# A two-layer hybrid block: how the RWKV-7 triangles of the second layer are inverted

## The chip, the cores and the metric

The kernel runs on one core of a Trainium2 chip. The metric is the time of one execution on the device, in microseconds (us), as the median of several runs.

## What is computed

The program is a backbone block of two layers on 256 context tokens and 256 latent tokens of width 1024. Each layer projects its normed input into three parallel mixers (mLSTM, RG-LRU, RWKV-7), gates and sums their outputs, and ends in a SwiGLU network. The part that matters here is the RWKV-7 scan, run over 16 heads of width 64 and in both directions:

```python
def step(s, x_t):
    r_t, w_t, k_t, v_t, kap_t, kapa_t = x_t
    s_kap = jnp.einsum('bhvk,bhk->bhv', s, kap_t)
    s = s * w_t[:, :, None, :] - s_kap[..., None] * kapa_t[:, :, None, :] + v_t[..., None] * k_t[:, :, None, :]
    return s, jnp.einsum('bhvk,bhk->bhv', s, r_t)
```

The latent scan starts from the final state of the context scan. Layer 1 returns both streams; of layer 2 only the latent stream is wanted, so its context half has no outputs.

## The kernel before

**Chunks and units.** The scan is cut into chunks of 32 tokens. Within a chunk the update is a triangular system: a strictly triangular 32x32 matrix per head, direction and chunk has to be inverted, and then a chunk is a few small matmuls. A *unit* u is four heads on one half of the tokens (even u: context, odd u: latent), in both directions, with eight chunks each, so each layer has eight units. Unit 2q+1 starts from the state that unit 2q leaves.

**The steps of a unit.** `rw_load` fetches its projected rows from DRAM. `rw_prep` builds decays and scaled keys, mostly on VectorE (L747 to L760). `chunks` (inside `rw_prep`) multiplies them on TensorE and masks the products into the tile `Am` on VectorE (L782): the triangles. It waits for the end of chain u-2, since `Am` has two buffers. Four or eight DMAs then write the triangles to a scratch in DRAM, `sc1` (L790, L793). `rw_tok` transposes keys and values. A *solve* inverts the triangles and brings the inverses back into `Am`. `rw_chain` then goes through the eight chunks, one after the other, each with a copy `xs` (L1102) near its start; its first instructions wait for the solve. `rw_tail` norms a unit's outputs and writes them.

**Two solves.** `rw_solve32` (layer 1) reads 64 triangles of 32x32, one on each of 64 partitions, and eliminates on GpSimd: for each of 30 columns one multiply (L1031) and one subtract (L1033). One DMA stores the inverse, four bring it into `Am` (L1043). `rw_solve16` (layer 2) reads only the two 16x16 diagonal blocks of each triangle, on 128 partitions, and eliminates 14 columns (L974, L976). A copy transposes one block (L980), two DMAs store, four load the transposed block `PT` (L989) and eight load the blocks into `Am` (L992). Then TensorE makes the missing off-diagonal block: 64 small matmuls of `PT` with `Am`, which the trace counts as 128 (L999), a masked copy `Z` on ScalarE (L1002), 64 matmuls of `Z` with `Am`, again counted as 128 (L1007), and four copies on ScalarE into `Am` (L1012).

**What sets the order.** `weave` (L296 on) is a planner that runs while the program is built. Tasks are generators that yield costs, waits and conditions; the planner keeps a clock of its own and writes out the order of every engine's instructions, SP's DMA queue and GpSimd's among them. The last task of the list is `products`: the large projections for the other mixers (tile `mm`, L260). It fills TensorE wherever no other task is ready, and goes first where fewer than `COLS[l]` matmul columns (3000 in layer 1, 2400 in layer 2) were issued in the last 3413 ns of the planner's clock. Preparations stand ahead of chains, chains ahead of fills. Each engine then runs in exactly that order; an instruction whose data is late holds everything behind it on its engine. In layer 2 about half of the fill products have 256 columns in place of 512.

**The switch.** `BLOCKED[l]` (L38) picks the solve in three places: the stores of the triangles (L788 and L791), the task that is spawned (L794) and the shape of the scratch (L831).

Of the kernel before, what the change touches and what calls it, by code (L numbers as in the profile page):

```python
# [34 lines left out]
COLS = [3000, 2400]  # L35
GDP = 1
ORD = [0, 0]
BLOCKED = [0, 1]  # L38
SL = 1000
SW = 230  # L40
PW = 1700
# [172 lines left out]
class KB:  # L214
# [446 lines left out]
    def rw_prep(self, l, u, ctx_out):  # L661
# [103 lines left out]
        def chunks(bks, sc1):  # L765
# [20 lines left out]
            for j in range(2):  # L786
                for x in range(2):
                    for k in range(2 if BLOCKED[l] else 0):  # L788
                        b = 64 * x + 32 - 32 * j + 16 * k
                        nc.sync.dma_start(out=sc1[k, x, j].rearrange("q s t -> s q t"), in_=Am[b:b + 16, j, :, :, 16 * k:16 * k + 16].rearrange("p d c t -> p (d c) t"))  # L790
                    if not BLOCKED[l]:  # L791
                        b = 64 * x + 32 - 32 * j
                        nc.sync.dma_start(out=sc1[x, j].rearrange("q s t -> s q t"), in_=Am[b:b + 32, j, :, :, 0:32].rearrange("p d c t -> p (d c) t"))  # L793
            yield ("spawn", (self.rw_solve32, self.rw_solve16)[BLOCKED[l]](l, u, Am, sc1))  # L794
            yield ("spawn", self.rw_tok(l, u, ctx_out, bks, bp, v, dict(kr=kr, Am=Am, PL=PL)))
# [34 lines left out]
        self.locks.discard("sm")  # L830
        sc1 = self.dr.tile([2, 2, 2, 16, 16, 16] if BLOCKED[l] else [2, 2, 16, 32, 32], F32, name="sc1")  # L831
        bks = [None, None]
# [1095 lines left out]
```

## Time and profile before

| | us |
|---|---|
| median of 3 runs | 2859.28 (2857.77 to 2861.8) |
| the profiled execution | 2865.19 |
| its span in the trace | 2863.5 |
| TensorE busy | 2669.4 (93%) |
| VectorE busy | 1733.0 (61%) |
| ScalarE busy | 1280.4 (45%) |
| GpSimd busy | 604.4 (21%) |

The span is the time from the first to the last instruction of the program in the trace. PE is TensorE, DVE VectorE, ACT ScalarE, POOL GpSimd, SP the engine whose queue issues most DMAs. A busy TensorE is not TensorE at its peak, since matmuls are pipelined and the time of one is counted from its start to its modelled end. PEclk is the granted share of TensorE's full clock of 2.4 GHz; it has two levels, 1.00 and 0.50, and a stretch shows their mean.

### The profile page before, as it was taken

Reading aid. Unit: us, or ns where it says so; the run is one execution under the profiler, and the core shown is the slowest. Engines: PE = TensorE matmul, PEld = TensorE weight load, DVE = VectorE, ACT = ScalarE, POOL = GpSimd, SP = SyncE. Lnnn points to the kernel's source line nnn. Section 1 sums busy time; section 2 is a strip of 40 time slices with the busy share of each in tenths; the row PEclk is TensorE's granted clock in tenths of the full one; section 3 lists DMA queues with packets and bytes.
Section 4 is the critical chain, followed back from the end, with each engine's and each line's share of the span. In section 5 each row is a group of like instructions: output and inputs, shape, how many; then the busy total and the mean of one; then the engine's idle time right before and its main releaser. Section 6 shows DMA issues by size and latency. Waiting matters only on the chain.

```text
span 2863.5 us, 75206 instructions
## 1 busy us (share of the span) xinstructions
PE 2669.4 (93%) x31560; PEld 2056.4 (72%) x31560; DVE 1733.0 (61%) x3762; ACT 1280.4 (45%) x2536; POOL 604.4 (21%) x983
## 2 busy tenths in 40 slices
PE   6998999999988999999999999999989998889998
PEld 4876677666644676777777877777767675589898
DVE  4677777785678524553333366656566567767564
ACT  4544444443377422342222254444444337755553
POOL 1056666565022000020000010222322201100000
PEclk9999999999999999999999999998999998999999
DMA  6543343434452557755554345433334345377564
GB/s 218 181 131 112 113 114 117 112 105 115 155 159 91 191 162 227 229 187 155 169 166 143 120 135 162 140 96 97 100 106 109 88 152 162 98 219 234 148 183 141
DMA packets 253716, 418.18 MB, mean 146 GB/s; under 512 B 95904, under 2 KB 145824, under 8 KB 253376
## 3 DMA queue, kind: packets, MB, share of 16 engines
q1 hardware_dynamic: 231344, 336.75, 38.7%
q10 hardware_dynamic: 22032, 76.61, 9.4%
q8 instruction: 248, 4.06, 0.6%
q14 instruction: 92, 0.75, 0.1%
HBM read 347.18 MB, written 65.04 MB: 144 GB/s over the span
## 4 chain that ended last, share of the span: by engine, by line
PE 70%; DVE 11%; DMA 7%; issue 5%; ACT 4%; POOL 3%; SPq 1%; ACTq 0%; POOLq 0%; DVEq 0%
PE mm L425 23%; PE mm L260 20%; PE mm L1591 8%; PE sm L260 6%; DMA wraw<-in_wA_dram 3%; PE sm L1429 2%; PE u L260 2%; PE sc L260 2%; PE xy L260 2%; PE xy L1248 2%; DVE wlo L473 1%; DMA yraw<-ysc 1%; PE sm L1525 1%; PE u L1550 1%; PE u L441 1%
## 5 line engine op out<-in xcount | busy, mean ns | idle before, releaser
L260 PE MATMUL mm<-hl,whi 128*128 128x512 f32 (+1 forms) x1184 | 456.4, 385 | 10.9 <-DVE stage L549 9.1
L260 PE MATMUL mm<-hh,whi 128*128 128x512 f32 (+1 forms) x1184 | 458.7, 387 | 0.0
L260 PE MATMUL mm<-hh,wlo 128*128 128x512 f32 (+1 forms) x1184 | 457.6, 386 | 0.3 <-issue 0.3
L383 DVE TENSOR_TENSOR wlo<-wraw,whi 128x512 fp32r<-128x512 f32 (+1 forms) x310 | 214.2, 694 | 287.0 <-ACT whi L382 283.9
L425 PE MATMUL mm<-hl,whi 128*128 128x512 f32 (+1 forms) x1056 | 368.6, 349 | 9.1 <-ACT whi L382 7.1
L425 PE MATMUL mm<-hh,wlo 128*128 128x512 f32 (+1 forms) x1056 | 362.0, 344 | 11.4 <-DVE wlo L383 11.3
L425 PE MATMUL mm<-hh,whi 128*128 128x512 f32 (+1 forms) x1056 | 360.7, 342 | 0.0
L382 ACT CAST whi<-wraw 128x512 fp32r<-128x512 f32 (+1 forms) x310 | 188.4, 614 | 346.0 <-PE mm L425 236.4
L473 DVE TENSOR_TENSOR wlo<-wraw,whi 128x512 fp32r<-128x512 f32 x296 | 225.8, 764 | 82.6 <-ACT whi L470 79.5
L260 PEld LDWEIGHTS mm<-hl,whi 128*128 128x128 f32 x1184 | 227.9, 192 | 60.2 <-issue 7.8
L260 PEld LDWEIGHTS mm<-hh,wlo 128*128 128x128 f32 x1184 | 227.9, 192 | 45.0 <-issue 3.1
L260 PEld LDWEIGHTS mm<-hh,whi 128*128 128x128 f32 x1184 | 227.9, 193 | 43.7 <-issue 1.0
L382 ACT CAST whi<-wx 128x512 fp32r<-128x512 f32 x212 | 128.8, 609 | 266.1 <-PE mm L425 164.7
L470 ACT CAST whi<-wraw 128x512 fp32r<-128x512 f32 x296 | 182.1, 617 | 139.4 <-PE mm L260 98.2
L425 PEld LDWEIGHTS mm<-hl,whi 128*128 128x128 f32 x1056 | 202.0, 191 | 58.5 <-ACT whi L382 25.5
L383 DVE TENSOR_TENSOR wlo<-wx,whi 128x512 fp32r<-128x512 f32 x212 | 144.6, 683 | 148.8 <-ACT whi L382 146.9
L425 PEld LDWEIGHTS mm<-hh,wlo 128*128 128x128 f32 x1056 | 201.8, 191 | 45.7 <-DVE wlo L383 13.7
L1277 POOL TENSOR_TENSOR nsq<-nsq,stage 128x256 f32<-128x256 f32 (+1 forms) x28 | 25.9, 926 | 954.1 <-ACT stage L1275 698.2
L425 PEld LDWEIGHTS mm<-hh,whi 128*128 128x128 f32 x1056 | 202.1, 191 | 22.9 <-issue 2.9
L1591 PE MATMUL mm<-ylo,whi 128*128 128x256 f32 (+1 forms) x544 | 183.7, 338 | 4.0 <-DVE ylo L383 3.8
L1591 PE MATMUL mm<-yhi,wlo 128*128 128x256 f32 (+1 forms) x544 | 179.9, 331 | 0.5 <-DVE wlo L383 0.2
L1591 PE MATMUL mm<-yhi,whi 128*128 128x256 f32 (+1 forms) x544 | 179.6, 330 | 0.0
(331 smaller groups left out, 5333.7 us busy)
## 6 DMA issues: line engine op xcount, KB each, us to landing
wraw<-in_wA_dram ACTq DMA_DIRECT2D x144, 512.0 KB, 4.1
wraw<-in_wA_dram SPq DMA_DIRECT2D x131, 512.0 KB, 4.3
wx<-in_wA_dram SPq DMA_DIRECT2D x81, 512.0 KB, 4.3
wx<-in_wM_dram SPq DMA_DIRECT2D x55, 512.0 KB, 3.9
wraw<-in_wM_dram SPq DMA_DIRECT2D x41, 512.0 KB, 3.8
mld<-stage SPq DMA_DIRECT2D x48, 256.0 KB, 3.9
wraw<-in_wB_dram SPq DMA_DIRECT2D x23, 512.0 KB, 3.4
pd<-stage SPq DMA_DIRECT2D x40, 256.0 KB, 3.8
```

The source lines that it names most:

```text
L260: self.nc.tensor.matmul(out, lhsT, rhs, start=start, stop=stop)
L382: self.nc.scalar.copy(hi[i], x[i])
L383: self.nc.vector.tensor_tensor(out=lo[i], in0=x[i], in1=hi[i].bitcast(F32), op=ALU.subtract)
L425: self.nc.tensor.matmul(ps, x[k], y[:, koff + k, t0:t0 + n], start=start and i == 0, stop=stop and i == 3 * nk - 1)
L441: self.nc.tensor.matmul(pss[n][:, t0:t1], w[x][:, k % 4], a[y][:, k, t0:t1], start=first and k == ks[0] and i == 0, stop=last and k == ks[ ...
L470: self.nc.scalar.copy(hi, x)
L473: self.nc.vector.tensor_tensor(out=lo, in0=x, in1=hi.bitcast(F32), op=ALU.subtract)
L1248: nc.tensor.matmul(ps[32 * q:32 * q + 32], self.cp[:, k], w[:, 256 * q:256 * q + 256], start=k == 0, stop=k == KC - 1)
L1429: nc.tensor.matmul(zp[R], lw[R, d, w], u[R], start=True, stop=True)
L1525: nc.tensor.matmul(ps[:, ts:], k[:, c, 128 * sb:128 * sb + 128], q[:, c, ts:], start=c == 0, stop=c == 1)
L1550: nc.tensor.matmul(ps, P[d][sb][:, 128 * tb:128 * tb + 128], v[:, sb], start=n == 0, stop=n == len(lst) - 1)
L1591: self.nc.tensor.matmul(ps, x[k], y[k][:, t0:t1], start=i == 0, stop=i == 3 * KC - 1)
```

## The change

One number changes: layer 2 takes `rw_solve32` in place of `rw_solve16`. Its triangles go to the scratch in four DMAs in place of eight, the elimination has 30 columns in place of 14, and the block product on TensorE, the transposed copy and the copies of ScalarE are gone. `COLS`, the planner's other constants and layer 1 stay as they are; the planner makes a new order for layer 2.

```diff
-BLOCKED = [0, 1]
+BLOCKED = [0, 0]
```

The function that layer 2 then calls, with what it issues:

```python
def rw_solve32(self, l, u, Am, sc1):
    ...
    N = re.tile([64, 32, 32], F32, name="N")
    nc.sync.dma_start(out=N, in_=sc1.rearrange("x h q s t -> (x h q) s t"))
    ...
    for i in range(1, 31):
        w = 31 - i
        ...
        G.tensor_tensor(out=tv, in0=N[:, 0:i, i:i + 1].broadcast_to([64, i, w]), in1=N[:, i:i + 1, i + 1:32].broadcast_to([64, i, w]), op=ALU.mult)
        ...
        G.tensor_tensor(out=N[:, 0:i, i + 1:32], in0=N[:, 0:i, i + 1:32], in1=tv, op=ALU.subtract)
    ...
    nc.sync.dma_start(out=sc2.rearrange("x h q s t -> (x h q) s t"), in_=N)
    ...
            nc.sync.dma_start(out=Am[b:b + 32, j, :, :, 0:32].rearrange("p d c t -> p (d c) t"), in_=sc2[hd, j].rearrange("q s t -> s q t"))
```

## Rows read from the trace of the kernel before

**Rows 1.** The page, part 1: busy time, share of the span, instructions.

```profile
PE 2669.4 (93%) x31560; PEld 2056.4 (72%) x31560; DVE 1733.0 (61%) x3762; ACT 1280.4 (45%) x2536; POOL 604.4 (21%) x983
```

**Rows 2.** Windows from first to last chain step, layer 1 then layer 2.

```profile
core 0: us, PE busy (x) PEld busy (x) DVE busy (x) ACT busy (x) POOL busy (x), PEclk, DMA share, GB/s
234.00:741.00 507.00, 481.51 (x9891) 346.31 (x9884) 373.57 (x871) 204.27 (x459) 300.10 (x453) 1.00 0.38 107
1839.00:2339.00 500.00, 461.43 (x10979) 357.82 (x10980) 305.77 (x815) 221.75 (x514) 114.03 (x235) 0.93 0.38 103
```

**Rows 3.** Timeline of VectorE, layer 2 (start us, us): triangles L782, chain steps L1102.

```profile
1839.56 0.28 DVE L1102 COPY xs<-xy 128x128 f32<-128x128 f32 x1
...
1862.72 0.68 DVE L782 TENSOR_TENSOR Am<-sm,cst 128x512 f32<-128x512 f32 x1
...
1895.67 0.29 DVE L1102 COPY xs<-xy 128x128 f32<-128x128 f32 x1 [0.78 <-PE xy L260]
...
2179.36 0.29 DVE L1102 COPY xs<-xy 128x128 f32<-128x128 f32 x1
...
2236.28 0.29 DVE L1102 COPY xs<-xy 128x128 f32<-128x128 f32 x1 [0.19 <-PE xy L260]
...
2241.43 0.69 DVE L782 TENSOR_TENSOR Am<-sm,cst 128x512 f32<-128x512 f32 x1 [0.77 <-PE sm L260]
...
2293.92 0.29 DVE L1102 COPY xs<-xy 128x128 f32<-128x128 f32 x1 [0.93 <-PE xy L260]
...
2324.96 0.29 DVE L1102 COPY xs<-xy 128x128 f32<-128x128 f32 x1 [0.67 <-PE xy L260]
```

**Rows 4.** Timeline of ScalarE, layer 2, units 5, 7: copies ending the solve.

```profile
2162.49 1.49 ACT L1012 COPY Am<-sm 16x256 f32<-16x256 f32 x4 [1.57 <-PE sm L260]
...
2286.97 1.49 ACT L1012 COPY Am<-sm 16x256 f32<-16x256 f32 x4 [2.56 <-PE sm L260]
```

**Rows 5.** Timeline of VectorE, layer 1: triangles of units 0, 1, 7, chain steps.

```profile
162.33 1.29 DVE L782 TENSOR_TENSOR Am<-sm,cst 128x512 f32<-128x512 f32 x2 [1.14 <-PE sm L260]
...
227.02 0.69 DVE L782 TENSOR_TENSOR Am<-sm,cst 128x512 f32<-128x512 f32 x1 [0.43 <-PE sm L260]
...
234.15 0.29 DVE L1102 COPY xs<-xy 128x128 f32<-128x128 f32 x1 [1.48 <-PE xy L260]
...
643.00 0.69 DVE L782 TENSOR_TENSOR Am<-sm,cst 128x512 f32<-128x512 f32 x1
...
711.56 0.29 DVE L1102 COPY xs<-xy 128x128 f32<-128x128 f32 x1 [1.72 <-PE xy L260]
```

**Rows 6.** Windows of tiles PT and Z, layer 2; PT's wait (us, times).

```profile
1800.00:2340.00 540.00, 12.34 (x1024) 10.93 (x1024) 0.93 0.38 105
...
1800.00:2340.00 540.00, 11.43 (x1024) 9.94 (x1024) 3.79 (x8) 0.93 0.38 105
...
  DMA Am<-sc: 10.6, 10
```

**Rows 7.** Lines of GpSimd, whole span: busy us, mean ns, idle before.

```profile
L1033 POOL TENSOR_TENSOR N<-N,et 64x30 f32<-64x30 f32 (+14 forms) x240 | 151.7, 632 | 18.7
...
L976 POOL TENSOR_TENSOR N<-N,et 128x14 f32<-128x14 f32 (+6 forms) x112 | 38.4, 343 | 8.8
```

**Rows 8.** Windows around the block products of units 0 and 7.

```profile
1828.00:1840.00 12.00, 9.14 (x290) 6.93 (x289) 6.95 (x17) 3.98 (x9) 0.00 (x0) 0.72 0.51 147
...
2279.00:2289.00 10.00, 6.63 (x310) 4.77 (x311) 2.12 (x7) 2.78 (x8) 0.00 (x0) 0.78 0.26 72
```

**Rows 9.** Lines of VectorE, layer 1 then layer 2: busy us, mean ns, idle.

```profile
L749 DVE SCALAR_TENSOR_TENSOR bk<-at,th 128x256 f32<-128x256 f32 x28 | 17.0, 611 | 0.0
...
L749 DVE SCALAR_TENSOR_TENSOR bk<-at,th 128x256 f32<-128x256 f32 x28 | 11.6, 418 | 0.0
```

**Rows 10.** Timelines of VectorE and TensorE at the tail of layer 2.

```profile
2334.47 0.69 DVE L1196 TENSOR_TENSOR Y<-Y,var 128x512 f32<-128x512 f32 x1 [0.33 <-POOL var L1194]
...
2338.45 1.15 PE L260 MATMUL sc<-cst,Y 128*64 128x64 f32 x32
```

## What the change was expected to do

> **What bounds the kernel now.** I read four views, in this order: the page, the windows over both mixers, the timelines of VectorE and ScalarE around the chain, and the weights' and matmuls' totals of the block product. The page says that TensorE is busy for 93% of the span [rows 1]. That alone would say: remove matmuls, gain time. The windows show that it is not that simple. Layer 2's chain stretch runs at a granted clock of 0.93 and layer 1's at 1.00, and yet the two last almost equally long, 500 and 507 us, although layer 2 has half as many output products [rows 2]. So something beside matmul work paces layer 2.
>
> The change touches only the way from the masked triangles `Am` (L782) to the first chain step of the same unit (L1102). I call this way the solve. The reader should follow two loops through it. In the **chain loop** unit u needs its solve, its triangles need the end of chain u-2, and a chain of eight steps follows: 56.1 us from first to last step in unit 0 and 56.9 us in unit 5 (first and last of six, which take 55 to 62) [rows 3]. In the **prep loop** the triangles of u also need the rows that VectorE builds, and these wait for the preparation of u-1. The triangles come when both loops have let them: from those of unit 1 (1862.72) to those of unit 7 (2241.43) six units take 378.7 us, 126.2 us for each two [rows 3].
>
> The solve itself is late only at the ends. In unit 5 the last block copy ends at 2163.98 and the chain starts at 2179.36, with 15.4 us to spare; in unit 7 the copy ends at 2288.46 and the chain starts 5.5 us later [rows 3, 4]. Unit 0 has no chain ahead of it, so there the solve is wholly on the path.
>
> **The change, part by part.** *Removed from TensorE:* 2 x 128 small matmuls (as the trace counts) in each of eight units, 12.34 + 11.43 = 23.8 us, and the waits for the DMAs that bring the inverted blocks back, 10.6 us [rows 6]. *Clock:* around the block products the granted clock is 0.72 in the first and 0.78 in the last of eight stretches, so one of the two levels, 1.2 GHz, is granted for part of each [rows 8]. Over the chain stretch 0.93 instead of 1.00 is worth 0.07 x 500 = 35 us of full-clock work [rows 2]; that is an upper bound for what can come back. In layer 1, whose solve has no matmuls, nothing of it is lost. Together at most 69 us of TensorE time becomes free. ScalarE loses 8 x (1 + 4) small copies and SP's queue goes from 23 to 10 issues in each unit (8+1+2+12 against 4+1+1+4, counted in the code). I cost both at nothing: ScalarE is at 222 of 500 us [rows 2], and no wait that I found ends on an SP issue.
>
> *Added to GpSimd:* 30 pairs of instructions in place of 14. The subtracts alone go from 38.4/8 = 4.8 us to 151.7/8 = 19.0 us a unit [rows 7], and the multiplies are as many and alike. GpSimd then holds about as much as in layer 1, 300 of 507 us instead of 114 of 500 [rows 2]: it does not become the bound by its share. The planner puts the few other GpSimd instructions (L812, L874, L1194) between those of the solve, so they wait for one instruction, not for a whole inversion. SP's store of the inverse waits for the last GpSimd instruction, and queued behind it stand the loads of the next unit and the stores of the fill products; layer 1 has that wait at full rate and loses nothing visible by it.
>
> *The way itself, from triangles to chain.* Layer 1 measures the new one directly: 234.15 - 162.33 = 71.8 us in unit 0 and 711.56 - 643.00 = 68.6 us in unit 7; the mean of the eight is 70.3, from 66.1 to 74.6 [rows 5]. Layer 2 now takes 2293.92 - 2241.43 = 52.5 us in unit 7 [rows 3]. **Term 1: +17.8 us** for the last unit, with bounds +13.6 and +22.1. The 15 us to spare in the middle units does not cover it there either, by a few us.
>
> *When unit 7's triangles come.* In the new chain loop two units take 70.3, plus a chain, plus the way from the last chain step to the triangles two units on, which is 2241.43 - 2236.28 = 5.1 us in unit 7 [rows 3]; I take 7, an estimate that leaves some delay for the other units. A chain loses the block product that is woven into it: 23.8/8 + 10.6/8 = 4.3 us, and up to 35/8 = 4.4 us of clock, so 57 becomes 48 to 52; I take 50.5. The sum is 128 against 126.2, so +1.7 for each of three pairs, +5 in all. Triangle 1 should come some 2 us early, since chain 0 starts later and leaves the engines to it. **Term 2: +3 us.** Lower bound: a chain of 45 and a way of 5 give 120, which is -19. Upper bound: layer 1's own pair, (643.00 - 227.02)/3 = 138.7 [rows 5], which is +37. I stay near layer 2's own value, because layer 1's units have twice as many outputs.
>
> *After that.* Chain 7 lasts 2324.96 - 2293.92 = 31.0 us [rows 3], with fill products between its steps. With up to 69 us of TensorE freed, the fills will have run out by then, the engine is near idle and its clock may fall: **Term 3: +2 us** (0 to +6). The tail's transposes now stand behind fills, at 2338.45 although `Y` is ready at 2334.47 + 0.69 = 2335.16 [rows 10]: **Term 4: -3 us** (0 at the other end). The next stage starts behind this tail as before, so the shift goes to the end of the program undiminished.
>
> **Sum:** 17.8 + 3 + 2 - 3 = +19.8 us. The profiled execution took 2865.19 us (span 2863.5), which is 5.9 above the median 2859.28. The shift is added to the median: **2879 us**, 0.7% slower.
>
> **A rule weighed against the rows.** VectorE's row-building instruction L749 takes 611 ns on average in layer 1 and 418 ns in layer 2, same shape [rows 9]. Twelve such instructions a unit (L747, L749, L751) would cost 12 x 0.193 = 2.3 us a unit, 14 us over six, if the prep loop is the later one. The Trainium skill's GPSIMD Engine Reference, section Specifications, says that GpSimd shares its SBUF interface with VectorE and that the two contend where a VectorE instruction has two inputs in SBUF; these rows agree. It speaks against this change, as more GpSimd time lies beside the same VectorE work.
>
> **Rivals.**
> *Faster: the freed matmul time decides.* Freed TensorE time shortens both loops, through steps that wait less behind fills and block products and through a full clock. For it speak the 69 us and the block products woven into every chain; against it, that layer 1, at full clock and without block products, needs 138.7 us for two units. It decides if a pair falls under 120 us: -19 - 2 + 17.8 - 1 = -4, and at 116 us -16, about 2843 us. Chance 0.17.
> *No change.* The pair falls to 120 to 123 us and eats term 1: -4 to +5, about 2860 us. Chance 0.18.
> *Slower as forecast,* a pair of 123 to 133 us, +5 to +35: chance 0.48.
> *Much slower: the prep loop becomes the later one.* GpSimd's contention lengthens the rows, as above, and the pair goes to layer 1's 138.7: 37 + 17.8 = +55, about 2914 us. It decides above some 133 us. For it: the row builder's 193 ns [rows 9], and that the trace does not tell the two loops apart. Against it: layer 2's even units build fewer rows. Chance 0.17.
>
> **Range and chances.** A measurement of this kernel can tell about 0.2% (5.7 us) from no change. Faster 0.17, same 0.18, slower 0.65. The range takes in the "no change" case, a little of the faster one and most of the last: 2850 to 2908 us.
>
> **What would show it.** Right: no granted clock below 1.00 at the solves of layer 2; triangles to chain near 70 us in every unit; chain 0 starting about 20 us later, near 1860; gaps ahead of most chains in which a chain waits for the load of its triangles; the fill products ending 30 us or more before the last chain step. Wrong: pairs of units under 120 us (then the chain was paced by TensorE), or a last chain step at or before 2325. If the ways from triangles to chain come out shorter than in layer 1 (say 60 us), term 1 is the failed one.

## The result and the profile after

| | before | after |
|---|---|---|
| median | 2858.53 us (4 runs) | 2881.70 us (4 runs, 2877.1 to 2885.24) |
| the profiled execution | 2865.19 | 2879.49 |
| its span | 2863.5 | 2877.7 |

The ratio of the two is 1.0071, with an interval of 1.0050 to 1.0092: 20 us slower (14 to 26), 23 by the medians, where 20 us and 2879 were forecast. The profiled execution of before lies 6.7 us above its median and that of after 2.2 below, so the two traces differ by 14.3 us only; the accounts below are between these two. The time came out as forecast, but the sum behind it did not: two of its steps failed by more than the whole sum, in opposite directions, so that the time fits is in good part luck.

Page of after, part 1, against [rows 1]:

```profile
PE 2655.8 (92%) x29512; PEld 2041.7 (71%) x29512; DVE 1800.3 (63%) x3762; ACT 1267.7 (44%) x2496; POOL 821.6 (29%) x1231
```

2048 matmuls are gone and TensorE is 13.6 us less busy; GpSimd has 217 us more. Windows of after, from first to last chain step of each layer, against [rows 2] (us, busy time of each engine, granted clock, DMA share, GB/s):

```profile
core 0: us, PE busy (x) PEld busy (x) DVE busy (x) ACT busy (x) POOL busy (x), PEclk, DMA share, GB/s
234.00:741.00 507.00, 481.75 (x9849) 346.57 (x9848) 370.47 (x866) 204.36 (x460) 302.34 (x453) 0.99 0.36 106
1859.00:2370.00 511.00, 449.93 (x9154) 346.92 (x9154) 359.45 (x795) 214.16 (x488) 301.34 (x450) 0.96 0.37 111
```

Layer 1 is as it was. Layer 2's chains last 511 us in place of the 486 from 1839 to 2325, and GpSimd now holds 301 us, as in layer 1. (The second window of [rows 2] reaches to 2339, 14 us past the last chain step of before at 2324.96; from first to last step the two layers of before lasted 507 and 485 us, not 507 and 500.) The timeline of VectorE shows where its units stand, against [rows 3] (start us, us):

```profile
1784.77 0.75 DVE L782 TENSOR_TENSOR Am<-sm,cst 128x256 f32<-128x256 f32 x2
...
1857.92 1.29 DVE L782 TENSOR_TENSOR Am<-sm,cst 128x512 f32<-128x512 f32 x2 [0.44 <-PE sm L260]
1859.72 0.28 DVE L1102 COPY xs<-xy 128x128 f32<-128x128 f32 x1
...
2063.71 0.29 DVE L1102 COPY xs<-xy 128x128 f32<-128x128 f32 x1
2069.35 0.76 DVE L782 TENSOR_TENSOR Am<-sm,cst 128x256 f32<-128x256 f32 x2 [1.15 <-PE sm L260]
...
2081.73 0.29 DVE L1102 COPY xs<-xy 128x128 f32<-128x128 f32 x1 [1.69 <-PE xy L260]
...
2272.90 0.29 DVE L1102 COPY xs<-xy 128x128 f32<-128x128 f32 x1 [0.80 <-PE xy L260]
2276.29 1.29 DVE L782 TENSOR_TENSOR Am<-sm,cst 128x512 f32<-128x512 f32 x2 [0.19 <-PE sm L260]
...
2323.34 0.29 DVE L1102 COPY xs<-xy 128x128 f32<-128x128 f32 x1 [0.99 <-PE xy L260]
2347.08 0.29 DVE L1102 COPY xs<-xy 128x128 f32<-128x128 f32 x1 [0.80 <-PE xy L260]
...
2370.04 0.29 DVE L1102 COPY xs<-xy 128x128 f32<-128x128 f32 x1 [0.20 <-PE xy L260]
```

Chain 0 starts at 1859.72, 75.0 us after its triangles and 20 us later than before. The triangles of unit 7 come at 2276.29, 34.9 us later, and the last chain step at 2370.04, 45.1 us later. Chain 7's first step has a hole in it, from 2323.34 to 2347.08. TensorE's timeline says what stood there (in brackets: idle time before, and what ended it):

```profile
2269.11 0.38 PE L425 MATMUL mm<-hl,whi 128*128 128x256 f32 x1
...
2338.75 0.39 PE L260 MATMUL u<-xs,Am 32*32 32x64 f32 x2 [14.94 <-DMA Am<-sc]
```

TensorE is idle for 14.94 us until the DMA brings the last inverse into `Am`: the unhidden rest of the solve. The first line is a product of the *next* stage, the gates of the merge (L425). It comes 101 us before the last chain step; in the kernel before the first of these stood 15 us after it:

```profile
2339.53 0.39 PE L425 MATMUL mm<-hl,whi 128*128 128x256 f32 x1
```

Windows from the last chain step to the first merge product (L1591), before and then after:

```profile
2325.00:2555.00 230.00, 192.27 (x1083) 137.72 (x1078) 167.74 (x377) 147.28 (x278) 26.28 (x53) 0.91 0.52 159
```

```profile
2370.00:2560.00 190.00, 151.00 (x791) 99.60 (x785) 147.75 (x340) 125.10 (x228) 25.68 (x53) 0.89 0.44 138
```

This stretch is 40 us shorter and holds 41 us less of TensorE's busy time: 29 us of gate products (53.5 in place of 82.4) and the 13 us of fill products that in before still ran after the last chain step. So of the 45 us only 5 reach the merge. The merge itself is then 10 us longer (104 us at a clock of 0.96 against 94 at 1.00), and what follows is as long as before: 14.2 us in the span.

### The profile page after: what moved, and what is told of

It reads as the page before. It is cut to its first block, busy times and chain, and to the rows that moved or that the text cites. A ratio compares the mean times of both kernels' runs of the same rounds, so it can differ in the third digit from the quotient of the medians.

```text
span 2877.7 us, 71160 instructions
## 1 busy us (share of the span) xinstructions
PE 2655.8 (92%) x29512; PEld 2041.7 (71%) x29512; DVE 1800.3 (63%) x3762; ACT 1267.7 (44%) x2496; POOL 821.6 (29%) x1231
## 4 chain that ended last, share of the span: by engine, by line
PE 67%; DVE 14%; issue 6%; DMA 6%; ACT 4%; POOL 3%; SPq 0%; ACTq 0%; DVEq 0%; POOLq 0%
PE mm L425 23%; PE mm L260 19%; PE mm L1591 7%; PE sm L260 5%; DVE wlo L473 2%; PE sm L1429 2%; PE sc L260 2%; PE u L260 2%; DMA wraw<-in_wA_dram 2%; DMA yraw<-ysc 2%; PE xy L1248 2%; PE xy L260 2%; PE sm L1525 1%; POOL N L1033 1%; PE u L441 1%
## 5 line engine op out<-in xcount | busy, mean ns | idle before, releaser
L425 PE MATMUL mm<-hl,whi 128*128 128x512 f32 (+1 forms) x1056 | 370.1, 351 | 7.9 <-ACT whi L382 6.0
L425 PE MATMUL mm<-hh,wlo 128*128 128x512 f32 (+1 forms) x1056 | 363.6, 345 | 10.9 <-DVE wlo L383 10.9
L425 PE MATMUL mm<-hh,whi 128*128 128x512 f32 (+1 forms) x1056 | 363.0, 344 | 0.0
L1033 POOL TENSOR_TENSOR N<-N,et 64x30 f32<-64x30 f32 (+14 forms) x480 | 304.0, 633 | 37.6
L1031 POOL TENSOR_TENSOR et<-N 64x30 f32<-64x30 f32 (+14 forms) x480 | 287.4, 599 | 60.6 <-DMA N<-sc 24.2
L473 DVE TENSOR_TENSOR wlo<-wraw,whi 128x512 fp32r<-128x512 f32 x296 | 244.1, 826 | 72.9 <-ACT whi L470 67.4
L425 PEld LDWEIGHTS mm<-hl,whi 128*128 128x128 f32 x1056 | 202.1, 191 | 58.3 <-ACT whi L382 23.7
L425 PEld LDWEIGHTS mm<-hh,wlo 128*128 128x128 f32 x1056 | 202.0, 191 | 45.7 <-DVE wlo L383 12.3
L425 PEld LDWEIGHTS mm<-hh,whi 128*128 128x128 f32 x1056 | 202.3, 192 | 25.0 <-issue 2.9
L1591 PE MATMUL mm<-ylo,whi 128*128 128x256 f32 (+1 forms) x544 | 185.1, 341 | 8.2 <-DVE ylo L383 8.1
```

Source lines behind the costliest of these rows:

```text
L425: self.nc.tensor.matmul(ps, x[k], y[:, koff + k, t0:t0 + n], start=start and i == 0, stop=stop and i == 3 * nk - 1)
L473: self.nc.vector.tensor_tensor(out=lo, in0=x, in1=hi.bitcast(F32), op=ALU.subtract)
L1031: G.tensor_tensor(out=tv, in0=N[:, 0:i, i:i + 1].broadcast_to([64, i, w]), in1=N[:, i:i + 1, i + 1:32].broadcast_to([64, i, w]), op=ALU.mult)
L1033: G.tensor_tensor(out=N[:, 0:i, i + 1:32], in0=N[:, 0:i, i + 1:32], in1=tv, op=ALU.subtract)
L1591: self.nc.tensor.matmul(ps, x[k], y[k][:, t0:t1], start=i == 0, stop=i == 3 * KC - 1)
```

## The experiments

Two questions: what holds the loop of units in layer 2 (the length of the solve, GpSimd's load on VectorE, or the fills on TensorE), and where 40 us went after it.

**The length of the solve.** The kernel after, with 14 of the 30 columns; the rest of the inversion is left out.

```diff
-        for i in range(1, 31):
+        for i in range(1, 15 if l else 31):
```

> The changed kernel, with layer 2's elimination on GpSimd ended after 14 of its 30 columns (the rest of the inversion is left out). Theory A (the length of the solve decides: in the changed kernel the triangles of unit u come 3 to 7 us after the last step of chain u-2, and from triangles to chain it takes 66 to 82 us): the way falls by about 22 us to some 54 us, as before the change, the chains follow one another, and with the block product gone the last step of chain 7 comes before 2325; the time falls below that of the kernel before, to 2820 to 2850 us. Theory B (the change costs through GpSimd's contention with VectorE or through the freed TensorE time being filled otherwise): GpSimd's time is about halved, so about half of the 23 us remain: 2866 to 2876 us.

Measured: 2798.57 us, ratio to before 0.9810 (0.9788 to 0.9833). Windows from its first to its last chain step:

```profile
1832.00:2282.00 450.00, 430.49 (x9170) 337.15 (x9175) 323.92 (x813) 211.78 (x484) 161.10 (x226) 0.99 0.40 125
```

The time lies below both ranges. The length of the solve decides, and further than expected: the stretch falls from 511 to 450 us at a clock of 0.99. With a solve no longer than the old one, the kernel without the block product on TensorE is 55 us faster than before. The edit also takes GpSimd's time in these windows from 301 to 161 us; the next run is there to tell the two apart.

**GpSimd's load alone.** The kernel before, with 48 more subtracts on GpSimd in each unit of layer 2, which nobody waits for.

```diff
+        yield ("spawn", self.rw_extra())
...
+        for i in range(48):
+            G.tensor_tensor(out=x[:, 32:160], in0=x[:, 32:160], in1=x[:, 0:1].broadcast_to([128, 128]), op=ALU.subtract)
```

> The kernel before, with 48 subtracts on GpSimd (128 x 128 elements, two inputs, a tile of their own, about 27 us a unit) behind each solve of layer 2, which nothing waits for. This is the GpSimd time that the change adds, without the longer solve. Theory A (length of the solve): VectorE's row-building instructions of layer 2 rise from 418 to about 500 to 600 ns, but the time moves by no more than 6 us: 2855 to 2865 us. Theory B (contention): most of the 23 us show here, 2870 to 2885 us.

Measured: 2848.14 us, ratio 0.9979 (0.9966 to 0.9993). The row builder's line in layer 2, in the kernel after and in this one (busy us, mean ns, idle):

```profile
L749 DVE SCALAR_TENSOR_TENSOR bk<-at,th 128x256 f32<-128x256 f32 x28 | 17.9, 641 | 0.1
```

```profile
L749 DVE SCALAR_TENSOR_TENSOR bk<-at,th 128x256 f32<-128x256 f32 x28 | 15.6, 558 | 0.1
```

Against 418 ns [rows 9] both are slower, and GpSimd's total is 801 us here and 822 in after. So the rows are slowed and the time is not (it is 2 to 10 us shorter): in the order of before this load costs nothing. The Trainium skill's GPSIMD Engine Reference, section Specifications, says that the two engines contend for their shared SBUF interface where VectorE's instruction has two inputs in SBUF; these rows agree.

**The elimination on two engines.** The kernel after, with columns 10 to 21 of layer 2's elimination on VectorE, where such an instruction takes 383 ns against 694 to 896 on GpSimd at these sizes.

```diff
+            onv = l and VS[0] <= i < VS[1]
+            E = self.nc.vector if onv else G
...
-            G.tensor_tensor(out=N[:, 0:i, i + 1:32], in0=N[:, 0:i, i + 1:32], in1=tv, op=ALU.subtract)
+            E.tensor_tensor(out=N[:, 0:i, i + 1:32], in0=N[:, 0:i, i + 1:32], in1=tv, op=ALU.subtract)
```

> The changed kernel, with 12 of the 30 columns of layer 2's elimination (the longest, 10 to 21) on VectorE in place of GpSimd. By the trace a pair of 230 elements takes about 1.6 us on GpSimd and, by VectorE's rows, about 0.8: some 10 us less from triangles to chain, some 10 us more VectorE time a unit. Theory A (length of the solve): two units are bound by way + chain, so 10 us less a unit end the last chain some 30 us earlier: 2835 to 2865 us. Theory B (VectorE, busy two thirds and slowed by GpSimd's contention, becomes the bound): 2875 to 2900 us.

Measured: 2904.48 us, ratio 1.0170 (1.0145 to 1.0194), outside what was expected. GpSimd's wait for VectorE's part of the tile `N`, in the seven units that are solved from the first chain step on (us, times; L1034 is the multiply there):

```profile
  POOL et L1034: 238.2, 7
```

GpSimd waits 34 us in each unit (23 to 46) for steps that take 64.3/7 = 9.2 us of VectorE's time: these steps stand in VectorE's queue behind rows and chain steps. The way from triangles to chain grows to 83 to 102 us in units 0 to 6 and the last chain step comes at 2406.5. A miss as a remedy; as a test it shows the same as the first, from the other side: a longer way, a later end, although GpSimd's time from first to last chain step is down to 162 us and the row builder (L750 in this kernel) is back at 444 ns.

**Where the 40 us went.** First the gate products of layer 2 cut to two of eight steps of their depth, in before and in after.

```diff
-                            K.gemm(ps[:, t0:], K.wblk(l, f"mg{b}_{j}"), h, t0, T - t0)
+                            K.gemm(ps[:, t0:], K.wblk(l, f"mg{b}_{j}"), h, t0, T - t0, nk=2 if l else KC)
```

> The kernel before, with 2 of 8 blocks of the inner dimension in the merge-gate products of layer 2 (three quarters of these products are left out). Taken with the next run. 24 x 18 matmuls of 256 columns less are 46 us at the full clock: 2815 to 2850 us.

> The changed kernel with the same cut in layer 2's merge gates. Theory (the changed chain ends 45 us later in the trace, but about 29 us of full-clock gate products of the next stage are run ahead inside the idle TensorE time of the last two chains): with three quarters of these products gone in both kernels there is little left to run ahead, and this run is 38 to 48 us slower than the one before it. Rival (the missing part comes back elsewhere, for instance in a less loaded next stage): the gap stays at 18 to 28 us.

Measured: 2851.46 us, ratio 0.9995 (0.9981 to 1.0009), and 2874.78 us, 1.0072 (1.0053 to 1.0090). The gap of 23 us is what the rival named, but the pair decides nothing, since the first run did not get faster either. The loads and splits of the gate weights were left in place, and its merge still begins 232 us after its last chain step, to set against the 230 us of before above:

```profile
2310.00:2542.00 232.00, 161.15 (x677) 94.70 (x676) 167.69 (x375) 146.79 (x276) 24.28 (x53) 0.74 0.50 156
```

TensorE is 31 us less busy there, at a clock of 0.74 in place of 0.91. So the edit was made again with them: only every fourth block of gates, with its loads, splits and products.

```diff
+                            if not l or j % 4 == 0:
+                                ps = K.mm()
+                                K.gemm(ps[:, t0:], K.wblk(l, f"mg{b}_{j}"), h, t0, T - t0)
```

> The kernel before, with only 6 of layer 2's 24 merge-gate products computed, loaded and split (the other 18 gates store a copy of one of the six). Cutting the inner dimension left the loads and splits of the weights in place; this takes them out too. Taken with the next run. Theory (in the changed kernel the gate products that stand between the last LRU and the first merge product were run ahead in the idle time of the last chains): in the kernel before, these take 36 us in the trace (from 2519 to 2555), and most of that goes: 2815 to 2835 us.

> The changed kernel with the same cut. Theory: its first merge product already follows the last LRU directly, so there is nothing to gain: 2865 to 2882 us, 40 to 55 us above the run before it, which is the 45 us by which the last chain ends later in the trace. Rival (the 31 us come back elsewhere): the gap stays at 18 to 28 us.

Measured: 2819.46 us, ratio 0.9868 (0.9844 to 0.9891), and 2857.81 us, 1.0006 (0.9991 to 1.0021). Last chain step and first merge product of the one, then of the other:

```profile
2320.64 0.29 DVE L1102 COPY xs<-xy 128x128 f32<-128x128 f32 x1 [0.67 <-PE xy L260]
...
2498.86 0.58 PE L1591 MATMUL mm<-ylo,whi 128*128 128x256 f32 x1 [4.28 <-DVE ylo L383]
```

```profile
2360.32 0.29 DVE L1102 COPY xs<-xy 128x128 f32<-128x128 f32 x1 [0.34 <-PE xy L260]
...
2531.36 0.58 PE L1591 MATMUL mm<-ylo,whi 128*128 128x256 f32 x1 [4.99 <-DVE ylo L383]
```

With most of the gate work gone the merge comes 178 and 171 us after the chain, in place of 230 and 190. Of the 39.7 us at the last chain step 32.5 now reach the merge and 32.1 the end of the two traces, where it was 5 of 45; by the medians the two kernels lie 38.3 us apart, not 23. So the gate work is most of what had filled the waiting time of the last chains: 33 of the 40 us. That is shown.

**The mirror: the block product in layer 1 too.**

```diff
-BLOCKED = [0, 1]
+BLOCKED = [1, 1]
```

> The kernel before with the 16x16 solve in layer 1 as well. Theory A (two loops: where chains wait for solves, the shorter solve pays; where TensorE is full, the block product costs): layer 1's chains wait for their solves (two units take 138.7 us), but its TensorE has 24 us idle in 507 and about 69 us would be added to it: slower, 2870 to 2910 us. Theory B (the length of the solve alone decides): layer 1 gains what layer 2 loses by the change, some 20 us: 2830 to 2845 us.

Measured: 2879.10 us, ratio 1.0081 (1.0059 to 1.0102), inside the 2870 to 2910 us of the first theory. Layer 1's last chain step, in this kernel and in before, and then this kernel's window to set against [rows 2]:

```profile
715.84 0.29 DVE L1102 COPY xs<-xy 128x128 f32<-128x128 f32 x1
```

```profile
740.62 0.29 DVE L1102 COPY xs<-xy 128x128 f32<-128x128 f32 x1
```

```profile
234.00:741.00 507.00, 473.96 (x11226) 344.85 (x11227) 315.02 (x863) 203.85 (x468) 110.92 (x239) 0.96 0.32 95
```

In layer 1 the shorter solve brings the last chain step 25 us *earlier*, and yet the time is 23 us longer: VectorE and GpSimd have less to do, the clock is 0.96 in place of 1.00, the fill products end at 796.8 instead of 759.2, and the first merge comes 25 us later. What moves with the time there is the end of TensorE's work and not the end of the chain. Each layer is better off with the solve that it had, for opposite reasons.

**Fewer fills in the chains.** `COLS[1]`, the planner's measure for how early a fill product goes first, halved, in after and in before.

```diff
-COLS = [3000, 2400]
+COLS = [3000, 1200]
```

> The changed kernel with COLS 1200 in place of 2400 in layer 2, so that fill products go ahead of chain and preparation only where fewer than half as many columns were issued lately. In the changed kernel the chains of units 1 to 5 still take 54 to 63 us, although the block product is out of them, and hold 24 to 27 us of fill products in place of 13 to 21. Theory F (the planner puts fills where the block product was, and they keep the chains long): chains fall to 50 to 55 us, two units to 128 to 134, the last chain ends 10 to 25 us earlier, and the time is 2858 to 2876 us. Rival (the chains are long by VectorE, which holds 49 to 56 us of them): chains stay at 55 to 63 and the time at 2876 to 2892 us.

> The kernel before with the same COLS, as the other half of that comparison. Its TensorE has fills to the end of the chains and after, so shorter chains would only move fills behind them: within 10 us, 2848 to 2866 us, with the last fill product later against the last chain step than the 13 us of before.

Measured: 2879.69 us, ratio 1.0061 (1.0039 to 1.0082), and 2869.78 us, 1.0033 (1.0013 to 1.0053). In after nothing changes, and the time is in the rival's range: middle chains of 53 to 61 us, TensorE busy with fills for 31 to 35 us of each where it was 32 to 36 (the 24 to 27 us of the expectation count their columns at 2.4 GHz), the last step at 2371.8. The fills seem to enter where the planner has nothing else ready, whatever their priority; since they did not get fewer, the run does not tell whether they hold the chains. The second run lies above its range, 7 us above its own before.

**The stall of the block product alone.** The kernel before, with the product planned 2.5 us later, so that it waits less for its operand.

```diff
-        yield ("wait", DMR + 1500)
+        yield ("wait", DMR + 4000)
```

> The kernel before, with the planner told that the inverted blocks land 2.5 us later, so that TensorE finds other work ahead of the block product in place of waiting (10.6 us of waits for these blocks in the trace of before, and part of the 82 us at half clock). Theory (the middle units have 10 to 17 us to spare between solve and chain, so a later product costs nothing there): TensorE's waits fall under 4 us, 2844 to 2854 us. Rival (units 0, 1 and 7 have none to spare and pay 2.5 us each, and order matters little): 2856 to 2866 us.

Measured: 2860.00 us, ratio 0.9993 (0.9974 to 1.0012). The wait for `PT`, to set against [rows 6] (us, times):

```profile
  DMA Am<-sc: 1.9, 3
```

The stall of 10.6 us is down to 1.9, and 20 us of half clock went with it (61.4 in place of 81.9 us between 1750 and the last chain step), and nothing is won. The time lies in the rival's range, and the ways of units 0, 1 and 7 are 1.5, 5.7 and 3.5 us longer than in before; whether TensorE's time counted for nothing or was paid back there, this run doesn't tell.

**The long solve where there was time to spare.** The kernel before, with the 32x32 elimination in units 4 and 6 alone, the tiles of both solves sharing buffers.

```diff
+LONG = (4, 6)
...
+        blocked = int(BLOCKED[l] and u not in LONG)
```

> The kernel before, with units 4 and 6 of layer 2 alone on the 32x32 elimination on GpSimd; the other six keep the 16x16 blocks with the block product. Both units lie in the middle of the layer, where the chain of the unit before still runs when the triangles are ready, so a longer solve of these two can be covered. Theory with two limits (the solve costs time only where a chain waits for it, TensorE's freed product counts only where TensorE has work to do): TensorE loses two block products, about 2 x 8.6 = 17 us at full clock, the last chain step moves by 0 to 5 us later, and the time is 2843 to 2857 us. Rival (any unit with the long solve shifts all that follow, since the buffers of the triangles turn with two units): two of seven steps of the loop lengthen by about 13 to 18 us each, a part is given back by the next stage's products, and the time is 2860 to 2875 us.

Measured: 2862.47 us, ratio 1.0018 (1.0005 to 1.0031), 1 to 9 us slower: no gain, and the low end of the rival's range. From the first to the last chain step it is 495.7 us against 485.4. The eight chains together last 417.9 us against 418.4, so no shortening by TensorE's freed product is seen; the waits ahead of chains 4 to 7 grow by 10.3 us together. A gain of a few us in the chains could hide here: both gate runs of before and the mirror, whose waits between the chains of layer 2 are those of before within 0.5 us, took 475 to 482 us for the stretch and 409 to 415 for the chains. The spare time of [rows 4] covers most of a longer solve but not all of it.

## Why the prediction was right, and where it was not

**Term 1 and the loop.** The prediction's loop can be measured term by term. Each row is the mean of units 1, 3 and 5, from the L782 and L1102 rows of both traces; the sum is the time from the triangles of one odd unit to those of the next. The other traces with layer 2 in the order of before give 123 to 125 us for it, those with the long solve on GpSimd in all units 137 to 140.

| us | before | predicted | after |
|---|---|---|---|
| the way, triangles to first chain step | 59.8 | 70.3 | 79.1 |
| chain, first to last step | 56.7 | 50.5 | 56.6 |
| last chain step to triangles | 9.8 | 7 | 3.8 |
| sum | 126.2 | 127.8 | 139.5 |

The structure was right for the kernel after: from unit 2 on, the triangles of unit u follow the last step of chain u-2 by 3 to 7 us, while the last of the rows that VectorE builds for them is ready 4 to 10 us ahead of that step, so the chain loop turns slower than the prep loop. In the kernel before it was the other way round for four of these six units: the rows of units 2, 3, 4 and 5 were ready 9.4, 8.7, 3.7 and 1.6 us *after* the last step of chain u-2. Unit 3 before, then after (last step of chain 1, last row of unit 3, its triangles):

```profile
1970.70 0.29 DVE L1102 COPY xs<-xy 128x128 f32<-128x128 f32 x1 [1.92 <-PE xy L260]
...
1979.02 0.42 DVE L755 TENSOR_TENSOR kr<-kr,pp 128x256 f32<-128x256 f32 x1
...
1986.33 1.29 DVE L782 TENSOR_TENSOR Am<-sm,cst 128x512 f32<-128x512 f32 x2 [1.47 <-PE sm L260]
```

```profile
1985.93 0.42 DVE L755 TENSOR_TENSOR kr<-kr,pp 128x256 f32<-128x256 f32 x1
...
1995.93 0.28 DVE L1102 COPY xs<-xy 128x128 f32<-128x128 f32 x1
...
1999.54 1.29 DVE L782 TENSOR_TENSOR Am<-sm,cst 128x512 f32<-128x512 f32 x2 [0.77 <-PE sm L260]
```

So the trace does tell the two loops apart, which the prediction said it does not. In these four units the longer solve moved the limit from the prep loop to the chain loop, and part of the 9.8 us from chain to triangles in the table is that wait for rows. Two sizes of the chain loop were wrong.

*The way is 79 us, not 70.* The elimination is the smaller part: from its load to its end it takes 49.2 us on average in units 1, 3 and 5, and 47.3 us in layer 1. From its end to the issue of the loads into `Am` it takes 12.1 us there against 4.3 in layer 1. Of these 7.8 us more, some 5 are waits in SP's queue, ahead of the store or after it has landed, and some 2.5 the store itself, which takes 8.4, 4.7 and 4.9 us to land where layer 1 has 3 to 5. The queue is at its worst in unit 3. Unit 3 of layer 2 after, then of layer 1 before (end of the elimination, then SP's issues):

```profile
2056.12 0.15 POOL L1035 MEMSET N<- 64x32 f32 x1
...
2060.40 0.55 SPq L1038 DMA_DIRECT2D sc<-N  x1
...
2072.47 3.48 SPq L793 DMA_DIRECT2D sc<-Am  x4
2076.00 2.09 SPq L1043 DMA_DIRECT2D Am<-sc  x4
```

```profile
418.04 0.46 SPq L1038 DMA_DIRECT2D sc<-N  x1
421.11 1.91 SPq L1043 DMA_DIRECT2D Am<-sc  x4
...
441.30 2.81 SPq L793 DMA_DIRECT2D sc<-Am  x4
```

In layer 1 the inverse is stored at once, loaded 3 us later, and the next unit's triangles are stored 20 us after that. In layer 2 the store comes 4 us late, behind the loads of a later unit and the store of a fill product, and the loads of the inverse stand *behind the stores of unit 4's triangles* (L793), which themselves wait for chain 2 and a masked product: 15.6 us from store to load, though the store had landed after 4.7. Chain 3 then starts 18 us after chain 2. In unit 1 it is the store that is slow; the loads go out as soon as it has landed, at 1927.59, and why it took 8.4 us no run shows:

```profile
1919.23 0.52 SPq L1038 DMA_DIRECT2D sc<-N  x1
...
1927.61 2.35 SPq L1043 DMA_DIRECT2D Am<-sc  x4
```

The prediction said that "no wait that I found ends on an SP issue" and costed the queue at nothing from layer 1. Layer 1's cover, triangles that come well after the inverse of the unit before, is gone in unit 3 of layer 2. The order is read from the trace; a kernel with these DMAs on another queue was not run, so what it would bring is open.

*The chains did not shorten.* The prediction took the block product and the half clock out of each (57 to 50.5). The product went, and most of the half clock: 38.2 us in chains 1, 3 and 5 together became 10.2. But the planner put fill products in the place: TensorE is busy with them for 32 to 34 us in chains 1, 3 and 5 where 24 to 28 had been, and VectorE is busy for 43 to 44 us in these chains, against 31 to 40. Which of the two holds a chain at 57 us stays open: fewer fills could not be had by their priority, and GpSimd's load was tried only in the order of before. The short elimination, with fewer of both in chains 1 and 3, has 52 us there and 57 in chain 5.

**Term 2** (+3 us for unit 7's triangles, bounds -19 to +37) is the mis-sized one: 34.9 us. That is three pairs of 139.46 - 126.24 = 13.2 us each, less 4.8 us by which unit 1's came earlier (2 were forecast). Of the 11.7 us by which a pair came out longer than the predicted 127.8, the way gives 8.8, the chain 6.1 and the lag -3.2. The pair has the size that the "much slower" rival gave for it, 138.7 us, and with it 2914 us, but not its reason: the rival blamed the prep loop and GpSimd's contention.

**Terms 1 and 3 at unit 7.** From its triangles to the last chain step it is 93.7 us against 83.5: +10.2, where 17.8 + 2 were forecast. The bare solve is longer about as said: from the triangles to the last block copy it was 47.0 us [rows 3, 4], and until the inverse is in place and the first product with it starts it is 62.5 now, +15.4. The row that I took for the end of the way hides this in unit 7: the chain's first copy `xs` doesn't need the inverse, and stands 15.4 us ahead of the product that waits for it. **Term 4** came as forecast: the transposes follow `Y` at once, at 2379.95 instead of 3.3 us behind it [rows 10], -3.1 us.

**The step that was missing.** "The shift goes to the end of the program undiminished" is wrong. The shift of the last chain step is +45, twice the 22.8 of terms 1 to 3; 40 of it are won back ahead of the merge, most of it by gate work that moved into the idle time of the last chains (shown by the pair without it), and 10 lost again in the merge. I had read that the fills would run out, and put down only the cost of an idle engine. The two errors nearly cancel, and so the time was right: the direction and the loop were reasoned, the size was luck.

**The signs.** Seen: chain 0 near 1860 (1859.72); the fills ending 30 us or more ahead of the last chain step (2268.6, 101 us ahead); gaps ahead of chains 1, 3 and 5 (16, 18 and 15 us). Partly: the ways are near 70 us, but from 72.9 to 82.2 in units 0 to 6. Not seen: a clock that stays at 1.00. It is half once in each of units 1 to 6, for 24 us together, and again from 2326 to 2344, around TensorE's wait for the last inverse; in all for 51.2 us between 1750 and the last chain step, against 81.9 before. The rival "freed matmul time decides" is what happens with a short solve (-55 us); with the long one no run shows a gain from TensorE's freed time.

## What to carry to other kernels

A busy share of 93% does not say that taking work from that engine gains time: write down the loop that a buffer closes (here triangles, solve, chain, and the triangles two units on), put a duration from the trace on each arc, DMA queues included, and see whether the freed engine stands on it. Do the same for the loop beside it: the longer one sets the pace, and here the change swapped the two in four units. When a path moves to another engine, read what is queued ahead of its stores and loads in the *new* order; a neighbour stage in which the same DMAs go out at once proves only that stage. And before adding a delay to the end of a program, look at what the next stage could do in the meantime: work without data from the late chain moves into the gap and gives a part back.

## What the runs showed of the hardware

VectorE's row-building instruction with two inputs (L749) goes in layer 2 from 418 to 641 ns as GpSimd's time over the chains goes from 114 [rows 2] to 301 us, at the same shape; such a load alone, 558 ns with subtracts that nobody waits for, cost no time. Instructions of 383 ns on VectorE took the place of 694 to 896 ns on GpSimd and made the solve slower, since GpSimd waited 23 to 46 us in each unit for them: for this serial chain of small steps an engine with little else to do was better than a faster one with much.
